# Scores for second-half queries only, another order of the seven products, and the last tile's last unit added in two column halves

## The chip, the cores and the metric

The kernel runs on one core of a Trainium2 chip. The metric is the device time of one execution in microseconds (us). A core has a matrix engine (TensorE: PE for its matmuls, PEld for its loads of the stationary operand), a vector engine (DVE), a scalar engine (ACT), a general engine (POOL) and DMA queues (SP issues most of the transfers here). Each engine works through its own instructions in the order of its program.

## The reference

One decoder layer over 512 tokens of width 1024, in float32:

```
x = LN1(ALPHA*x + 0.5*SwiGLU_1(x))           # width 2816
q, f, i, g, conv_val, conv_gate = split(x @ w_in)
f = lb + (1-lb)*sigmoid(f);  k = 1 - f        # 4 heads, state 128x128
o[t] = sum over s <= t of ( sum_c q[t,c]*k[s,c]*prod of f[r,c] for s < r <= t ) * i[s]
A = rmsnorm(o) * gain * sigmoid(g)
B = silu(LN(causal_conv31(conv_val*sigmoid(conv_gate))))
x = LN2(ALPHA*x + concat(A, B) @ w_out)
x = LN3(ALPHA*x + 0.5*SwiGLU_2(x))
```

The reference writes the recurrence chunk by chunk; the sum above is what it comes to.

## The kernel before

**Feed-forward stages.** `ffn` is called twice. Gate and up weights come as "quads" of 128 features in four 512 x 128 quarters. The first two feature blocks are computed plainly. For the other nine (f = 2 to 10), times gate and up (s = 0, 1), a `Pair` computes a 2 x 2 block product by seven products (p1 to p7) instead of eight. One product is four steps of three matmuls (L407), each with 128 x 128 weights and 256 moving columns, in the float32r type: high and low parts, three of the four cross terms. So a pair is 84 matmuls, and the two calls hold 36 pairs. The order is the tuple `USUAL`. p1, p7 and p5 open an accumulation and ACT copies their sum out of the bank (L427); p2, p4 and p3 then go on accumulating onto p1, p7 and p5, so their first weight load waits for that copy. While a pair runs, the quad of the pair after the next is prepared: ACT casts its four operands to high parts (L68), DVE takes the low parts (L76) and forms sums (L143, L149, L150). A cast goes into a weight buffer that a product of the present pair must have left: b11/b21 are used by p1 and p2, t1/t3 by p5 and p7, t4/t2 by p4 and p6, b22 (tile w2hi) by p3. PE's order is written out by hand there; the order on ACT and DVE comes from the framework's scheduler.

**Down and output projections.** `rows_out` keeps four banks (128 tokens each, 512 columns). The last four units of weights are run tile by tile, then `add` (L330, L331) adds the bank to the residual and takes statistics, and `norm` finishes the tile's layer norm.

**Scores.** `scores(hp)` handles two heads at a time (hp = 0, 1). The decays are folded into q and k level by level. First come the scores with no decay (only the diagonal is kept), then for block sizes m = 1, 2, 4, ... 64: scores of every 128-token group, 128 x 128 (`score`, L773), of which only the entries are kept whose query lies in the second half of a block of 2m and whose key lies in the first half of the same block. They are kept by DVE with a mask for m up to 8 (L781, L813 `copy_predicated` into `diag`) and by ACT copies for 16 to 64 (L816). Each level then multiplies q's second halves and k's first halves by totals of f (L805) and forms the totals of the next level (L809). m = 128 and 256 are scores between groups (L792, L796). A score is a float32 matmul, and the trace shows two records for each: 2 heads x 4 groups x 2 = 16 records in a level.

Between two levels PE is given other matmuls by `weave`: 2.6 or 1.9 us (`IDLE`) of an estimated cost, in steps of three float32r matmuls of 512 columns. For hp = 0 these are gated(2), gated(3) and rows(value), while DVE also works on the convolution (L756); for hp = 1 they are rows(gate), and from the fourth step on the conv norm (`conv_norm`: transposes, bn_stats L859, rstd by POOL, L864) is called between levels too.

Of the kernel before, what the change touches and what calls it, by code (L numbers as in the profile page):

```python
# [9 lines left out]
F32 = mybir.dt.float32  # L10
# [7 lines left out]
P = 128  # L18
# [35 lines left out]
def decoder_layer(ctx, tc, x_tok, x_q, w_first, vec, bcast, ng, w_gu1, w_d1, w_i, w_g, w_col, w_o, w_gu2, w_d2, out):  # L54
# [138 lines left out]
    def mm3(ps, lh, ll, rh, rl, first, last):  # L193
        nc.tensor.matmul(ps, lhsT=lh, rhs=rh, start=first, stop=False)  # L194
        nc.tensor.matmul(ps, lhsT=lh, rhs=rl, start=False, stop=False)  # L195
        nc.tensor.matmul(ps, lhsT=ll, rhs=rh, start=False, stop=last)  # L196
# [13 lines left out]
    masks = const.tile([P, len(MASKED) + 1, P], U8, name="masks")  # L210
# [102 lines left out]
    def rows_out(ks, per, lhs, accs, factor, late, finish, follow=(), before=lambda u: None, then=lambda: None):  # L313
# [5 lines left out]
        stats = [small.tile([P, 2, 6], F32, tag="stats", name="stats") for _ in range(NT)]  # L319

        def part(acc, u, hi, lo, i):
            for j in range(per):
                n = per * u + j
                h, l = lhs(ks[n])
                mm3(acc[i], h[:, i * P:(i + 1) * P], l[:, i * P:(i + 1) * P],
                    hi[:, j, :], lo[:, j, :], n == 0, n == len(ks) - 1)

        def add(acc, half, i):
            z = xres[i][:, half * 512:(half + 1) * 512]
            nc.vector.scalar_tensor_tensor(z, acc[i], factor, z, op0=ALU.mult, op1=ALU.add)  # L330
            nc.vector.bn_stats(stats[i][:, half, :], z)  # L331
# [22 lines left out]
        for i in range(NT):  # L354
            add(acc, 0, i)
# [84 lines left out]
    USUAL = ("p1", "p7", "p2", "p4", "p5", "p6", "p3")  # L440
# [29 lines left out]
    def ffn(x, begun, gb_i, finish, follow=(), then=lambda: None, later=lambda: None):  # L470
        with tc.tile_pool(name="ffn", bufs=1) as fp:
# [33 lines left out]
            with tc.manual_schedule(engines={PE}):  # L505
# [8 lines left out]
                for f in range(PLAIN, NP):  # L514
                    h.append(h_of(f))
                    for s in range(2):
                        ahead(3)
                        w = unit_now()
                        ahead(3)
                        pr = Pair(PAIR_BANKS[f % 2][s], work_tile() if s else h[f])  # L520
                        for n in USUAL:
                            run(pr.steps(x, w, (n,)))
                            if f == PLAIN and s == 0 and n == "p7":
                                x.last_sum()
                        gate_up(s, pr)
# [91 lines left out]
    def make_masks():  # L617
# [4 lines left out]
        for n, m in enumerate(MASKED):  # L622
# [11 lines left out]
                                    fill=0.0, base=0, channel_multiplier=0)  # L634
            nc.gpsimd.tensor_copy(masks[:, n, :], mf)
        nc.gpsimd.tensor_copy(masks[:, len(MASKED), :], ident)
# [24 lines left out]
    with tc.tile_pool(name="mix", bufs=1) as mp:  # L661
# [56 lines left out]
        def forget_query(h):  # L718
# [7 lines left out]
            def query(ps):  # L726
                nc.scalar.copy(qk[h // 2][:, 0, h % 2, :], ps)
# [3 lines left out]
        us = {}  # L731
# [32 lines left out]
        def scores(hp):  # L764
            x = qk[hp]
            xf = x.rearrange("p a h t -> p (a h t)")
            q, k = x[:, 0], x[:, 1]

            def score(n, h):
                ps = bank(nbank[h][n % 2], NT, P)  # L770
# [3 lines left out]
                return ps  # L774

            yield IDLE[hp]
            both = [score(0, h) for h in range(2)]
            f = fq[:, 2 * hp:2 * hp + 2, :]
            nc.vector.tensor_tensor(q, q, f, op=ALU.mult)
            for h in range(2):  # L780
                nc.vector.copy_predicated(diag[h], masks[:, len(MASKED):, :].broadcast_to([P, NT, P]), both[h])  # L781
            yield IDLE[hp]
            tot = f.rearrange("p h t -> p (h t)")
            for n, m in enumerate(MASKED + COPIED + (128, 256)):
                if m <= 64:
                    both = [score(n + 1, h) for h in range(2)]
                else:
                    both = [bank(nbank[h][(n + 1) % 2], NT, P) for h in range(2)]
                for h, ps in enumerate(both):
                    if m == 128:  # L790
# [3 lines left out]
                    elif m == 256:  # L794
# [11 lines left out]
                if m < 128:  # L806
                    tt = tot.rearrange("p (b two) -> p b two", two=2)
# [3 lines left out]
                for h, ps in enumerate(both):  # L811
                    if m in MASKED:
                        nc.vector.copy_predicated(diag[h], masks[:, n:n + 1, :].broadcast_to([P, NT, P]), ps)  # L813
                    elif m <= 64:
                        for b in range(0, P, 2 * m):
                            nc.scalar.copy(diag[h][b:b + m, :, b + m:b + 2 * m], ps[b:b + m, :, b + m:b + 2 * m])  # L816
# [80 lines left out]
        with tc.manual_schedule(engines={PE}):  # L897
# [12 lines left out]
            bl += [mp.tile([P, T], F32R, name=f"bl{n}") for n in range(1, NC)]  # L910
# [94 lines left out]
```

## Time and profile before

| what | value |
|---|---|
| time, median of 3 runs | 942.77 us (942.49 to 943.42) |
| the profiled execution's own time | 942.62 us |
| its span, first to last instruction | 940.6 us |
| PE busy | 931.2 us, 99% |
| DVE busy | 679.8 us, 72% |
| ACT busy | 388.2 us, 41% |
| DMA, mean | 103 GB/s |
| granted TensorE clock, mean | 0.998 of 2.4 GHz |

The profiled execution is 2.0 us longer than its span (what lies around the first and the last instruction) and 0.15 us below the median. Records of matmuls overlap, since they are pipelined: the cost of one is read from start to start, not from its duration.

### The profile page before, as it was taken

How to read it: one execution, taken by the hardware profiler on the slowest of the kernel's cores; microseconds unless marked ns; L12 is line 12 of the kernel's file. 1: busy time of each engine (PE TensorE's matmuls, PEld its weight loads, DVE VectorE, ACT ScalarE, POOL GpSimd, SP SyncE). 2: the span in 40 equal slices, each digit the busy share in tenths (PEclk: the TensorE clock that was granted, in tenths of full speed). 3: DMA queues.
4: the chain of work that ended last, by engine and by line, in shares of the span. 5: the costliest groups of instructions: out<-in, count | busy, mean ns of one | idle time of the engine just before them, and what ended most of it. 6: DMA issues, size and time to landing. Idle time of an engine off the chain costs nothing.

```text
span 940.6 us, 14283 instructions
## 1 busy us (share of the span) xinstructions
PE 931.2 (99%) x5913; PEld 844.0 (90%) x5913; DVE 679.8 (72%) x933; ACT 388.2 (41%) x560; POOL 119.3 (13%) x142
## 2 busy tenths in 40 slices
PE   9999999999999999999999999999999999999996
PEld 6899999999888889888888888989999999988885
DVE  6988888887724265999887768958888888742417
ACT  5554455555421123414341723535555544721100
POOL 0000000000820015642462201000000000000001
PEclk9999999999999999999999999999999999999999
DMA  8522322324432313321140241213233222452302
GB/s 278 202 106 90 133 92 95 131 69 146 141 106 90 94 41 101 125 71 64 48 128 5 65 168 64 109 65 115 91 102 123 90 91 90 136 156 90 98 15 89
DMA packets 22464, 96.67 MB, mean 103 GB/s; under 512 B 2496, under 2 KB 3648, under 8 KB 17024
## 3 DMA queue, kind: packets, MB, share of 16 engines
q1 hardware_dynamic: 22320, 95.50, 30.4%
q8 instruction: 46, 0.75, 0.3%
q0 software_dynamic: 80, 0.26, 0.1%
q14 instruction: 18, 0.15, 0.1%
HBM read 93.66 MB, written 2.10 MB: 102 GB/s over the span
## 4 chain that ended last, share of the span: by engine, by line
PE 98%; DVE 2%; POOL 0%; issue 0%; DVEq 0%; ACT 0%
PE bank L407 39%; PE bank L196 18%; PE bank L194 18%; PE bank L195 18%; PE bank L773 2%; PE bank L830 1%; PE bank L578 0%; PE bank L796 0%; PE bank L288 0%; PE bank L274 0%; DVE qk L805 0%; DVE diag L813 0%; PE bank L792 0%; PE bank L847 0%; DVE cn L864 0%
## 5 line engine op out<-in xcount | busy, mean ns | idle before, releaser
L76 DVE TENSOR_TENSOR wlo<-raw,whi 128x1024 fp32r<-128x1024 f32 (+2 forms) x150 | 173.5, 1163 | 148.2 <-ACT whi L68 148.1
L68 ACT CAST whi<-raw 128x1024 fp32r<-128x1024 f32 (+2 forms) x172 | 173.2, 1012 | 258.0 <-PE bank L196 150.7
L194 PE MATMUL bank<-whi,hp 128*128 128x512 f32 x320 | 124.7, 390 | 0.0
L196 PE MATMUL bank<-whi,hp 128*128 128x512 f32 x320 | 124.5, 389 | 0.0
L195 PE MATMUL bank<-wlo,hp 128*128 128x512 f32 x320 | 124.5, 389 | 0.0
L407 PE MATMUL bank<-bh,whi 128*128 128x256 f32 x432 | 122.3, 283 | 0.0
L407 PE MATMUL bank<-bl,whi 128*128 128x256 f32 x432 | 122.3, 283 | 0.0
L407 PE MATMUL bank<-ah,whi 128*128 128x256 f32 x432 | 122.2, 283 | 0.0
L407 PE MATMUL bank<-ah,wlo 128*128 128x256 f32 x432 | 122.2, 283 | 0.0
L407 PE MATMUL bank<-al,whi 128*128 128x256 f32 x432 | 122.2, 283 | 0.0
L407 PE MATMUL bank<-bh,wlo 128*128 128x256 f32 x432 | 122.1, 283 | 0.0
L756 DVE SCALAR_TENSOR_TENSOR bank<-u,vecs,bank 128x512 f32<-128x512 f32 x120 | 81.2, 748 | 2.8 <-ACT bank L751 1.8
L407 PEld LDWEIGHTS bank<-bh,whi 128*128 128x128 f32 x432 | 82.9, 192 | 0.0
L407 PEld LDWEIGHTS bank<-bl,whi 128*128 128x128 f32 x432 | 82.9, 192 | 0.0
L407 PEld LDWEIGHTS bank<-bh,wlo 128*128 128x128 f32 x432 | 82.9, 192 | 0.0
L407 PEld LDWEIGHTS bank<-al,whi 128*128 128x128 f32 x432 | 82.8, 192 | 0.1
L407 PEld LDWEIGHTS bank<-ah,whi 128*128 128x128 f32 x432 | 82.7, 192 | 0.1
L407 PEld LDWEIGHTS bank<-ah,wlo 128*128 128x128 f32 x432 | 82.8, 192 | 0.0
L222 POOL TENSOR_TENSOR rstd<-rstd,negh 128x1 f32<-128x1 f32 (+1 forms) x18 | 17.9, 997 | 497.4 <-DVE rstd L221 497.4
L76 POOL TENSOR_TENSOR wlo<-raw,whi 128x256 fp32r<-128x256 f32 x88 | 66.5, 789 | 63.3 <-ACT whi L68 61.4
L195 PEld LDWEIGHTS bank<-wlo,hp 128*128 128x128 f32 x320 | 60.1, 188 | 12.5
L196 PEld LDWEIGHTS bank<-whi,hp 128*128 128x128 f32 x320 | 60.1, 188 | 12.4
(192 smaller groups left out, 1923.2 us busy)
## 6 DMA issues: line engine op xcount, KB each, us to landing
raw<-w_gu SPq DMA_DIRECT2D x42, 1024.0 KB, 4.8
raw<-w_d SPq DMA_DIRECT2D x44, 512.0 KB, 3.5
raw<-w_col SPq DMA_DIRECT2D x16, 512.0 KB, 3.5
raw<-w_o SPq DMA_DIRECT2D x8, 512.0 KB, 3.5
xres<-x_tok SPq DMA_DIRECT2D x4, 512.0 KB, 7.9
gb<-bcast SPq DMA_DIRECT2D x4, 512.0 KB, 5.1
raw<-w_i SPq DMA_DIRECT2D x4, 512.0 KB, 3.4
raw<-w_g SPq DMA_DIRECT2D x4, 512.0 KB, 3.5
```

Source lines behind the costliest of these rows:

```text
L68: nc.scalar.copy(hi, raw)
L76: engine.tensor_tensor(lo[..., sl], raw[..., sl], hi.bitcast(F32)[..., sl], op=ALU.subtract)
L194: nc.tensor.matmul(ps, lhsT=lh, rhs=rh, start=first, stop=False)
L195: nc.tensor.matmul(ps, lhsT=lh, rhs=rl, start=False, stop=False)
L196: nc.tensor.matmul(ps, lhsT=ll, rhs=rh, start=False, stop=last)
L222: nc.gpsimd.tensor_tensor(r, r, negh.broadcast_to([P, n]) if n > 1 else negh, op=ALU.pow)
L407: nc.tensor.matmul(ps, lhsT=l[:, k, :], rhs=r[:, k, :], start=first and k == 0 and j == 0, stop=k == 3 and j == 2, skip_group_check=True)
L756: nc.vector.scalar_tensor_tensor(accs[n], us[n][:, j:j + T], vecs[:, w:w + 1], accs[n], op0=ALU.mult, op1=ALU.add)
L773: nc.tensor.matmul(ps[:, g, :], lhsT=k[:, h, sl], rhs=q[:, h, sl], start=True, stop=True)
L830: nc.tensor.matmul(ps[:, i, :], lhsT=s, rhs=v[:, j, (2 * hp + h) * P:(2 * hp + h + 1) * P], start=(j == 0), stop=(j == i))
```

## The change

**Scores.** Every level's matmul takes only the queries that the level keeps. The diagonal's scores are taken with the 64 even queries of each group only. m = 1 and m = 2 share one matmul of 128 moving columns: the odd queries (kept apart by ACT in a new tile `odd`, [.., 0, :]) and, in [.., 1, :], the queries of m = 2. From m = 4 on a matmul has 64 moving columns (the second halves' queries, a strided operand) and 128 - m stationary ones. The number of matmuls in a level stays the same; there is one level less in a pair of heads (seven instead of eight with L773's work). The mask copies (`select`) write 256 elements per partition instead of 512; the diagonal's odd entries come with the mask of m = 1, to which the identity is added. DVE gets more and smaller multiplications in the first two steps; `scores` yields ten times instead of eleven, so the first part of the conv norm comes after m = 4 instead of after m = 2, and its last part after m = 256 instead of m = 128. The query evacuation is two ACT copies of 256 columns instead of one of 512.

**Order of products.** p7, p1, p4, p5, p2, p6, p3 in every pair but those of the last feature block, which keep p1, p7, p2, p4, p5, p6, p3.

**Last tile.** In each of the three `rows_out`, the last tile's last unit is run as two column halves (12 matmuls of 256 columns for 6 of 512), and the last tile's `add` works on 256 columns at a time.

```diff
-                for n, (u, hi, lo) in enumerate(kept):
+                for n, (u, hi, lo) in enumerate(kept[:-1]):
                     part(acc, u, hi, lo, i)
...
+                for c in range(0, 512, wide[i]):
+                    part(acc, *kept[-1], i, slice(c, c + wide[i]))
...
-                add(acc, 1, i)
+                for c in range(0, 512, wide[i]):
+                    add(acc, 1, i, c)
...
-    USUAL = ("p1", "p7", "p2", "p4", "p5", "p6", "p3")
+    USUAL, LAST = ("p7", "p1", "p4", "p5", "p2", "p6", "p3"), ("p1", "p7", "p2", "p4", "p5", "p6", "p3")
...
-                        for n in USUAL:
+                        for n in USUAL if f < NP - 1 else LAST:
...
-                nc.scalar.copy(qk[h // 2][:, 0, h % 2, :], ps)
+                p2 = ps.rearrange("p (t two) -> p t two", two=2)
+                nc.scalar.copy(qk[h // 2][:, 0, h % 2, :].rearrange("p (t two) -> p t two", two=2)[:, :, 0], p2[:, :, 0])
...
+                nc.scalar.copy(odd[-1][:, h % 2, :, 0, :], p2[:, :, 1].rearrange("p (g t) -> p g t", g=NT))
...
-                    nc.tensor.matmul(ps[:, g, :], lhsT=k[:, h, sl], rhs=q[:, h, sl], start=True, stop=True)
+                    nc.tensor.matmul(ps[:, g, 0:64], lhsT=k[:, h, sl],
+                                     rhs=q[:, h, sl].rearrange("p (t two) -> p t two", two=2)[:, :, 0],
+                                     start=True, stop=True)
...
+            nc.vector.tensor_tensor(k2[..., 0], k2[..., 0], f2[..., 1], op=ALU.mult)
...
+                    nc.tensor.matmul(ps[:, g, :], lhsT=k[:, h, g * P:(g + 1) * P],
+                                     rhs=w[:, h, g].rearrange("p a t -> p (a t)"), start=True, stop=True)
...
+                    if m <= 64:
+
+                        for g in range(NT):
+                            nc.tensor.matmul(ps[0:P - m, g, 0:64].rearrange("p (b m) -> p b m", m=m),
+                                             lhsT=k[:, h, g * P:(g + 1) * P - m],
+                                             rhs=halved(q, m, 1)[:, h, g * 64 // m:(g + 1) * 64 // m],
+                                             start=True, stop=True)
...
-                        nc.vector.copy_predicated(diag[h], masks[:, n:n + 1, :].broadcast_to([P, NT, P]), ps)
+                        select(h, ps[:, :, 0:64], n, m, 1)
```

## Rows read from the trace of the kernel before

**Rows 1.** The page: busy time by engine; shares of the chain that ended last.

```profile
PE 931.2 (99%) x5913; PEld 844.0 (90%) x5913; DVE 679.8 (72%) x933; ACT 388.2 (41%) x560; POOL 119.3 (13%) x142
PE 98%; DVE 2%; POOL 0%; issue 0%; DVEq 0%; ACT 0%
```

**Rows 2.** Stretches: busy us by engine (instructions), clock, DMA share, GB/s.

```profile
49.20:232.60 183.40, 183.40 (x1514) 182.34 (x1513) 154.94 (x208) 96.52 (x145) 1.31 (x3) 1.00 0.31 106
...
489.50:529.60 40.10, 39.76 (x259) 35.24 (x258) 28.98 (x50) 12.52 (x30) 8.54 (x10) 1.00 0.09 27
```

**Rows 3.** Chain in order of time, merged: start us, us, what.

```profile
49.35 183.22 PE bank L407 x1512
...
404.01 1.78 PE bank L773 x16
...
443.87 1.73 PE bank L796 x8
```

**Rows 4.** Timeline: one level of scores with hp 0, one with hp 1.

```profile
403.85 1.95 PE L773 MATMUL bank<-m 128*128 128x128 f32 x16
...
505.43 0.39 PE L196 MATMUL bank<-whi,xl 128*128 128x512 f32 x1
...
505.88 1.86 PEld L773 LDWEIGHTS bank<-qk 128*128 128x128 f32 x16 [0.48 <-DVE qk L805]
505.88 2.05 PE L773 MATMUL bank<-qk 128*128 128x128 f32 x16
```

**Rows 5.** Timeline of the first feed-forward stage: p6 ends, p3 begins.

```profile
137.91 1.05 ACT L68 CAST whi<-t 128x1024 fp32r<-128x1024 f32 x1 [1.83 <-PE bank L407]
...
138.86 0.37 ACT L427 COPY h<-bank 128x256 f32<-128x256 f32 x1
...
139.15 0.28 PE L407 MATMUL bank<-bh,wlo 128*128 128x256 f32 x1
139.28 0.19 PEld L407 LDWEIGHTS bank<-ah,w2hi 128*128 128x128 f32 x1
...
139.39 0.19 PEld L407 LDWEIGHTS bank<-al,w2hi 128*128 128x128 f32 x1
```

**Rows 6.** Waits between engines: us in total, times, longest.

```profile
PEld bank L773 <- DVE qk L805: 1.2, 2, 0.7
```

**Rows 7.** Timeline of DVE, one masked level with hp 1, first and last.

```profile
503.99 0.73 DVE L813 COPY_PREDICATED diag<-masks,bank 128x512 f32<-128x512 uint8 x1
...
508.83 0.73 DVE L813 COPY_PREDICATED diag<-masks,bank 128x512 f32<-128x512 uint8 x1
```

**Rows 8.** Groups of DVE, shapes apart.

```profile
L813 DVE COPY_PREDICATED diag<-masks,bank 128x512 f32<-128x512 uint8 x16 | 11.7, 729 | 1.0 <-PE bank L773 1.0
...
L429 DVE TENSOR_TENSOR h<-h 128x256 f32<-128x256 f32 x18 | 7.5, 417 | 0.0
```

**Rows 9.** Timeline of ACT: the four silus that end the conv norm.

```profile
527.59 2.93 ACT L888 ACTIVATE c<-c,vecs 128x512 f32<-128x512 f32 x4
```

**Rows 10.** Groups of PE, shapes apart: busy us, mean ns of one.

```profile
L407 PE MATMUL bank<-ah,w2hi 128*128 128x256 f32 x144 | 44.2, 307 | 0.0
L407 PE MATMUL bank<-al,w2hi 128*128 128x256 f32 x144 | 40.5, 281 | 0.0
```

**Rows 11.** Timeline of ACT, first half of the pair after that.

```profile
142.45 0.37 ACT L427 COPY work<-bank 128x256 f32<-128x256 f32 x1 [0.88 <-PE bank L407]
...
143.87 0.84 ACT L492 ACTIVATE h<-h 128x768 f32<-128x768 f32 x1
144.61 0.36 ACT L427 COPY work<-bank 128x256 f32<-128x256 f32 x1
```

**Rows 12.** Chain at the end of the span.

```profile
932.56 0.24 PE bank L196
...
932.82 0.70 DVE xres L330
...
933.55 0.70 DVE stats L331
```

More of the change, by code (lines that the diff above doesn't have):

```diff
@@ L191, in decoder_layer, with mm3 @@
     plan([w_d2[h, u] for h in range(2) for u in range(NP)], tok, nc.vector)
[L193 to L196, printed above, removed]
+    def mm3(ps, lh, ll, rh, rl, first, last, **kw):
+        nc.tensor.matmul(ps, lhsT=lh, rhs=rh, start=first, stop=False, **kw)
+        nc.tensor.matmul(ps, lhsT=lh, rhs=rl, start=False, stop=False, **kw)
+        nc.tensor.matmul(ps, lhsT=ll, rhs=rh, start=False, stop=last, **kw)
     def slot(tag, shape, dtype, name):
@@ L318, in rows_out, with part @@
         n_units = len(ks) // per
-        stats = [small.tile([P, 2, 6], F32, tag="stats", name="stats") for _ in range(NT)]
-        def part(acc, u, hi, lo, i):
+        wide = [512] * (NT - 1) + [256]
+        stats = [small.tile([P, 1024 // n, 6], F32, tag=f"stats{n}", name="stats") for n in wide]
+        def part(acc, u, hi, lo, i, cols=slice(0, 512)):
             for j in range(per):
@@ L767, in scores, with banks_of, halved, select @@
             q, k = x[:, 0], x[:, 1]
-            def score(n, h):
-                ps = bank(nbank[h][n % 2], NT, P)
+            w = odd[hp]
+            turns = [0]
+            def banks_of():
+                turns[0] ^= 1
+                return [bank(nbank[h][1 - turns[0]], NT, P) for h in range(2)]
+            def halved(t, m, k):
+                return t.rearrange("p g (b two m) -> p g b two m", two=2, m=m)[:, :, :, k]
+            def select(h, ps, n, m, k):
+                r = slice(0, P - (m if m > 2 else 0))
+                mask = masks[:, n:n + 1, :].broadcast_to([P, NT, P])
+                nc.vector.copy_predicated(halved(diag[h], m, k)[r], halved(mask, m, k)[r],
+                                          ps.rearrange("p g (b m) -> p g b m", m=m)[r])
@@ L771, in score @@
+            yield IDLE[hp]
+            both = banks_of()
+            for h, ps in enumerate(both):
                 for g in range(NT):
                     sl = slice(g * P, (g + 1) * P)
-                    nc.tensor.matmul(ps[:, g, :], lhsT=k[:, h, sl], rhs=q[:, h, sl], start=True, stop=True)
-                return ps
-            yield IDLE[hp]
-            both = [score(0, h) for h in range(2)]
-            f = fq[:, 2 * hp:2 * hp + 2, :]
-            nc.vector.tensor_tensor(q, q, f, op=ALU.mult)
@@ new lines, in scores @@
+            f4, q4, k4 = (t.rearrange("p (s t r) -> p s t r", s=2 * NT, r=4)
+                          for t in (fq[:, 2 * hp:2 * hp + 2, :].rearrange("p h t -> p (h t)"),
+                                    xf[:, 0:2 * T], xf[:, 2 * T:4 * T]))
+            f2, k2 = (t.rearrange("p s t (a b) -> p s (t a) b", b=2) for t in (f4, k4))
+            tot = totals[:, 0, :]
+            w0, w1 = (w[:, :, :, i, :].rearrange("p h g (t a) -> p (h g) t a", a=2) for i in range(2))
+            t4 = tot.rearrange("p (s t a) -> p s t a", s=2 * NT, a=2)
@@ new lines, in scores @@
+            nc.vector.tensor_tensor(q4[..., 1], w0[..., 0], t4[..., 0], op=ALU.mult)
+            yield IDLE[hp]
+            both = banks_of()
+            for h, ps in enumerate(both):
+                for g in range(NT):
+                    nc.tensor.matmul(ps[:, g, :], lhsT=k[:, h, g * P:(g + 1) * P],
+                                     rhs=w[:, h, g].rearrange("p a t -> p (a t)"), start=True, stop=True)
+            two = lambda t: t.rearrange("p (b two) -> p b two", two=2)
+            nc.vector.tensor_tensor(q4[..., 2:4], w1, t4[..., 0:1].broadcast_to([P, 2 * NT, 32, 2]), op=ALU.mult)
@@ L909, in decoder_layer @@
             bl = [parts.tile([P, T], F32R, tag="w2lo", name="bl0", bufs=2)]
-            bl += [mp.tile([P, T], F32R, name=f"bl{n}") for n in range(1, NC)]
+            b12 = mp.tile([P, 2, T], F32R, tag="odd", name="bl1")
+            bl += [b12[:, 0, :], b12[:, 1, :], mp.tile([P, T], F32R, name="bl3")]
             fill = rows(gate)
```

59 lines of the change are left out of this document (36 added, 23 removed).

## Prediction

> **What bounds the kernel now.** I read the page first: PE is busy for 99% of the span, every other engine for 72% or less, and the chain that ended last runs through PE for 98% [rows 1]. So only three things can move the time: the number and pitch of PE's instructions, the short stretches in which PE waits, and the tail after its last matmul. Then the busy times by stretch: in the first feed-forward stage PE has no gap and DVE is busy 155 of 183 us, in the scores of the second pair of heads PE loses 0.3 us [rows 2]. This understates the loss, because a matmul's record can begin while its weights are still being loaded; I therefore took the cost of a matmul from start to start. The merged chain gives that pitch directly: 1512 matmuls of 256 float32r columns take 183.22 us, 0.121 each; sixteen score records of 128 float32 columns 1.78 us, 0.111 each; eight records of 256 columns 1.73 us, 0.216 each [rows 3].
>
> **Scores: columns against loads.** The pitches [rows 3] say that the pitch of a float32 record follows its moving columns, 0.108 us per 128 plus a little. Taken alone they promise half the price for 64 columns. But every score record has its own weight load, which runs beside the matmul before it, and it can hide only as long as that matmul lasts. Its length shows where nothing hides it. With hp = 1, one level's load had to wait for DVE; its first matmul's record begins with the load, and the sixteen records cover 2.05 us instead of the 1.95 of an undisturbed level: 0.10 more [rows 4]. In the feed-forward stage an exposed load of 128 columns begins at 139.28 and the next one at 139.39 [rows 5], that is, the first took 0.11 until its matmul could run. So a load of 128 float32 columns costs about 0.107 us, just what 128 moving columns hide and twice what 64 will hide (0.054). My reading: for the 64-column records the load sets the pitch, and halving the moving columns alone gains nothing.
>
> What is left of the gain is one level less, and the narrower loads from m = 4 on. Before, a pair of heads pays 8 x 1.78 = 14.24 us. After, the diagonal and the joint level (128 columns each way) cost 1.78 each. m = 4, 8, 16, 32, 64 have 124, 120, 112, 96, 64 stationary columns. No row shows a load narrower than 128, so their price lies between 1.78 (a load costs the same however narrow) and 0.89 (it is no bound, half the columns cost half). I take it in proportion to the columns, my estimate from the 0.107 for 128: 1.73 + 1.67 + 1.56 + 1.34 + 0.89 = 7.19. Four of the five are near 128 columns, so they stay near the upper row in any case. The sum is 3.56 + 7.19 = 10.75, 3.5 us less for each pair of heads, **7.0 us less** in all. The ends: with loads of constant price 7 x 1.78 = 12.46, 3.6 us less in all; with loads that are no bound 6 x 0.89 + 1.78 = 7.12, 14.2 us less in all. The strided moving operand could cost up to twice a contiguous one without leaving this, since 2 x 0.054 is the load's time again.
>
> On the narrow loads the Trainium skill (page "TensorE: Matmul & The Clock Gate", section "LDWEIGHTS (loading the stationary operand)") says that a load takes its number of columns divided by 1.2 in ns, whatever the number of rows. That gives 107 ns for 128 columns, as the exposed loads here show, and 53 ns for 64. By it the five levels come to about 7.0 us, next to my 7.19, and it speaks against the full halving, which is rival 1 below.
>
> **Scores: waits.** PE waited twice for DVE with hp = 1: its load's idle time is 1.2 us in two waits, the longer 0.7 [rows 6]. The shorter one, 0.48, holds what is usual: the load began 0.45 after the last fill matmul's start at 505.43 [rows 4], where 0.23 is one pitch of 512 columns, so 0.22 was lost. The longer one by the same subtraction loses 0.44. Each also exposes a load, 0.10. Together 0.86 us. The cause is a level in which DVE has two masked copies, the multiplications and the conv norm: from 503.99 to 508.83, 4.84 us from one level's first masked copy to the next [rows 7]. A masked copy of 512 elements takes 0.73 and an operation of 256 elements 0.42 [rows 8], so two halves give DVE about 0.62 back: 4.2 us. PE's level is then 1.67 for the scores at m = 8, nine fill matmuls of 0.23, and four transposes of about 0.11: 4.2 as well. Moreover the conv norm now begins after m = 4, so only m = 8 has both masked copies and norm. I take **0.8 us less**; the ends are 0.9 (all waits gone) and 0 (they stay).
>
> The extra DVE operations of the first two steps cost me nothing: what must lie between the diagonal's matmuls and the joint ones is only one multiplication of 512 elements (about 0.7 us), under 2.1 us of fill; the rest depends on f and the odd queries alone. If that cover went, each step would cost PE some 0.5 us, four times. The second ACT copy of each query (about 0.4 us) hides behind the 5 us of the next column unit. The conv norm's last part comes one level later: its silus take 2.93 us [rows 9], its copies and splits perhaps 3 more, and PE still has nine fill matmuls, forty records of `values` at 0.11 and the fill's leftover, some 8 us. Bound 0 to 1, taken 0.
>
> **Order of the products.** The record of p3's first high part shows the stall: its 144 matmuls average 307 ns, the neighbouring ones 281 [rows 10]. 144 x 26 ns = 3.74 us, or 0.104 for each of the 36 pairs: once per pair a load is exposed. Why: when p5 ends, ACT begins a 1.05 us cast into the buffer that p5 left (137.91), and only then copies p5's sum (138.86 to 139.23). p6 covers 12 x 0.121 = 1.45 us, its last matmul starts at 139.15, and p3's load, which waits for the copy, begins at 139.28 instead of directly behind that matmul's start [rows 5]. Lateness is 0.01 and the exposed load 0.10, 0.115 per pair. In the new order p2 and p6 lie between p5 and p3, 2.9 us, and the same copy is over a good microsecond early. What is late next? p4 follows p7 with only p1 between. A first product's copy begins 142.45, about 1.7 us after the pair's start, and ends at 142.82 [rows 11]; p4's first load is due 2.9 us after the start, at 143.6: 0.8 to spare. The second product's copy is the one behind the silus (144.61 to 144.97) [rows 11]; that is p1's now, and p2 waits for it only at 5.8 us. The last feature block keeps its order, so 32 of 36 stalls go: **3.7 us less**. Ends: 0 (the stall moves to p4) and 4.1 (all).
>
> **Last tile.** 12 matmuls of 256 columns at 0.121 for 6 of 512 at 0.227 make each unit 0.09 us longer, three times. In the first two `rows_out` PE has other work behind it, nothing else changes: +0.2. At the end DVE starts 0.26 us after the last matmul's start and takes 0.70 + 0.70 plus gaps [rows 12]; with halves of about 0.36 the first half's two operations run under the second half's matmuls, and 0.75 us stand behind the last matmul instead of 1.46, and the last matmul is shorter by 0.1. Less the 0.09 that is 0.6 to 0.7 gained. Net **0.4 us less** (0 to 0.6).
>
> **Sum.** 7.0 + 0.8 + 3.7 + 0.4 = 11.9 us. The profiled execution's own time is 942.6 (span 940.6 and 2.0 around it), 0.15 below the median of the runs, so I forecast 942.8 - 11.9 = 930.9, rounded 931.0, span near 929.
>
> **Rivals.**
> 1. Loads are no bound and half the columns cost half. For it: the pitch of 128 and 256 columns [rows 3]; against it: the exposed loads [rows 4, 5]. Scores then give 14.2 less instead of 7.0, but PE's level with hp = 1 falls to 3.4 us where DVE needs up to 4.2, which takes back about 1.2: 931.0 - 7.2 + 1.2 = 925.0.
> 2. A load costs the same however narrow: 931.0 + 3.4 = 934.4. No row excludes it.
> 3. The stall only changes its place: p4 waits for p7's copy by a hair in each pair, as p3 did: 931.0 + 3.7 = 934.7. For it: ACT's order is the scheduler's, and a cast may again go before the copy; against it: 0.8 us to spare.
> 4. Slower than before: ACT takes a cast (1.05) and the pair's silus (0.84 and the smaller one, 1.1 in all) before p7's copy. Then the copy ends 1.7 + 2.2 + 0.4 = 4.3 us after the start, p4 is 1.4 late and pays 0.1 for the load; in the 16 pairs with silus that is 24 us, in the other 16, with a cast alone, 0.4 each, 6 us: 931 + 30 = 961. It decides from 0.37 us per pair on (11.9 / 32). For it: DVE is 85% busy there [rows 2], so the silus' time may shift; against it: silus start 1.1 us after the first product's copy today [rows 11].
>
> **How the numbers follow.** Forecast 0.55, with a range of its own from 929 to 933; rival 1 0.14; rival 2 0.10; rival 3 0.12; rival 4 0.06; a mishap that I don't see and that leaves no change 0.03. The range reaches from just below rival 1 to above rival 3, 924.5 to 936.0, and leaves about 0.1 out. A measurement of this kernel tells about 0.2%, 1.9 us, from no change. All cases but the last two are faster by more: 0.91; within 0.03; slower 0.06.
>
> **What would show it.** Right: score blocks of sixteen records at 1.78 for the diagonal and the joint level and falling from 1.73 to 0.9 for m = 4 to 64; p3's first matmul no longer with a mean of its own; no PE wait on L805's successor; some 0.7 us less after the last matmul. Wrong: blocks of 0.9 us already at m = 4 (rival 1) or of 1.78 at m = 64 (rival 2); p4's first matmul with a longer mean (rivals 3 and 4); PE gaps behind DVE in the first two steps of scores.

## The result, and the profile after

| what | before | after |
|---|---|---|
| time, median | 942.76 us | 935.15 us (934.90 to 935.56) |
| ratio after / before | | 0.9919 [0.9901, 0.9936] |
| span of the profiled execution | 940.6 us | 933.1 us |
| PE busy | 931.2 us | 923.2 us |

The change makes the kernel 7.6 us faster, 4.2 us short of the forecast: inside the whole range (924.5 to 936.0), outside the 929 to 933 that the forecast had for itself. The starts of PE's matmuls in the two traces, stage by stage, say where the time came from and where some went back. The third column is the forecast's term.

| stage (matmul start to matmul start) | after - before, us | forecast |
|---|---|---|
| ahead of the first product | -0.2 | |
| seven products, two stages | -1.55, -1.56 | -3.7 |
| down projection, first stage | **+0.70** | +0.1 |
| scores hp = 0 | -2.99 | -3.5 |
| scores hp = 1 with its waits | -3.33 | -4.3 |
| transposes behind the norm of the gate | **+0.54** | 0 |
| output projection | 0.0 | +0.1 |
| down projection, second stage | **+0.91** | +0.1 |
| behind the start of the last matmul | -0.04 | -0.7 |

The page of the kernel after, busy time by engine and shares of the chain, beside [rows 1]:

```profile
PE 923.2 (99%) x5899; PEld 836.8 (90%) x5899; DVE 673.8 (72%) x953; ACT 384.1 (41%) x564; POOL 120.8 (13%) x142
PE 90%; DVE 4%; issue 3%; POOL 2%; DMA 1%; ACT 1%; DVEq 0%; POOLq 0%; ACTq 0%
```

PE is still the bound. The chain now passes through other engines for 10% instead of 2%. Partly PE really waits for DVE (below); the rest I take for work of other engines that ended just in time, since PE's busy share is the same 99%.

**The levels of the scores** stand in the chain of the kernel after (start us, us, what), hp = 0, beside the 1.78 of [rows 3]:

```profile
402.95 1.73 PE bank L807 x16
...
407.50 1.78 PE bank L831 x16
...
412.02 1.68 PE bank L849 x16
...
416.54 1.63 PE bank L849 x16
...
420.95 1.53 PE bank L849 x16
```

L807 is the diagonal (64 moving columns, 128 stationary), L831 the joint level (128 each), L849 the levels from m = 4. The diagonal moves half the columns and pays all but the full price; m = 4, 8, 16 come down with their 124, 120, 112 stationary columns. This is the picture that the forecast drew from one exposed load.

**The products.** The groups of L414 (formerly L407) for p3's high part; the numbers behind the count are the least, median and greatest duration in ns:

```profile
L414 PE MATMUL bank<-ah,w2hi x144: 283/283/385, 57.6 to 804.2; 128*128 128x256 f32 x144
L414 PE MATMUL bank<-al,w2hi x144: 277/283/283, 57.7 to 804.3; 128*128 128x256 f32 x144
```

The two have the same median, and [rows 10] showed 307 against 281 as means; 385 is the stall in the second pair of the last feature block, which keeps the old order. The first pair of that block keeps it too and has no stall any more. The second pair has a new one, where p2 begins: two steps of 0.15 and 0.22 us instead of 0.12, 0.13 us more in each stage.

**A new wait in the scores.** The chain with hp = 1 ahead of the level m = 4:

```profile
490.65 0.52 DVE qk L834
491.17 0.33 DVE totals L837
491.50 0.64 DVE diag L798
492.14 0.04 DVE rstd L221
492.17 0.74 DVE diag L798
492.91 0.53 DVE qk L835
493.44 0.04 issue
493.49 1.95 PE bank L849 x16
```

PE's level hangs on L835 (k's multiplication by the totals of m = 1 and 2), which stands behind two mask copies (L798) of the same step. From the last fill matmul's start to the level's first start 0.69 us pass instead of 0.23, so 0.46 us are lost, and the first load is exposed, 0.10 more. The groups of DVE say why; the last two numbers before the idle time are busy us and mean ns:

```profile
L798 DVE COPY_PREDICATED diag<-masks,bank 128x256 f32<-128x256 uint8 x12 | 8.5, 738 | 0.0
L798 DVE COPY_PREDICATED diag<-masks,bank 120x256 f32<-120x256 uint8 x4 | 1.7, 428 | 0.2 <-PE bank L849 0.2
L798 DVE COPY_PREDICATED diag<-masks,bank 124x256 f32<-124x256 uint8 x4 | 1.7, 428 | 0.0
```

Halving a mask copy saves time only from m = 4 on (428 ns). For the diagonal, m = 1 and m = 2, with every second element or pairs, 256 elements take 738 ns, as long as 512 did (729, [rows 8]).

**A new wait behind the values.** Timeline of POOL, and of PE's loads (rows of two answers):

```profile
530.21 1.65 POOL L222 TENSOR_TENSOR rstd<-rstd,negh 128x8 f32<-128x8 f32 x1 [14.07 <-DVE rstd L221]
531.83 1.29 POOL L726 TENSOR_TENSOR m<-m,ngb 128x512 f32<-128x512 f32 x1
...
534.11 0.53 PEld L910 LDWEIGHTS bank<-ident,m 128*128 128x128 f32 x5 [0.49 <-DVE m L906]
```

The last row of the gate reaches POOL so late that its multiplication (L726) stands behind the 1.65 us of the power for rstd (L222); DVE's L906 waits for it, and PE's transposes for DVE.

**The tail.** The chain at the end, beside [rows 12]:

```profile
925.06 0.13 PE bank L196
925.19 0.02 issue
925.22 0.76 DVE xres L333 x2
925.97 0.67 DVE stats L334 x2
926.64 0.02 issue
926.66 0.27 DVE mv L339
```

Both halves of the addition begin behind the last of the twelve matmuls: 1.43 us of DVE, before 0.70 + 0.70.

### The profile page after: what moved, and what is told of

Same layout as the page of the kernel before. It is cut to its first block, busy times and chain, and to the rows that moved or that the text cites. A ratio compares the mean times of both kernels' runs of the same rounds, so it can differ in the third digit from the quotient of the medians.

```text
span 933.1 us, 14256 instructions
## 1 busy us (share of the span) xinstructions
PE 923.2 (99%) x5899; PEld 836.8 (90%) x5899; DVE 673.8 (72%) x953; ACT 384.1 (41%) x564; POOL 120.8 (13%) x142
## 4 chain that ended last, share of the span: by engine, by line
PE 90%; DVE 4%; issue 3%; POOL 2%; DMA 1%; ACT 1%; DVEq 0%; POOLq 0%; ACTq 0%
PE bank L414 39%; PE bank L194 16%; PE bank L196 16%; PE bank L195 16%; DVE bank L771 2%; PE bank L849 1%; POOL wlo L76 1%; PE bank L274 0%; PE bank L288 0%; DMA raw<-w_g 0%; DMA xr<-x_q 0%; DVE diag L798 0%; DVE bl L954 0%; DVE m L906 0%; PE bank L920 0%
## 5 line engine op out<-in xcount | busy, mean ns | idle before, releaser
L414 PE MATMUL bank<-ah,whi 128*128 128x256 f32 x432 | 122.5, 283 | 0.0
L414 PE MATMUL bank<-bl,whi 128*128 128x256 f32 x432 | 122.3, 283 | 0.0
L414 PE MATMUL bank<-ah,wlo 128*128 128x256 f32 x432 | 122.2, 283 | 0.0
L414 PE MATMUL bank<-al,whi 128*128 128x256 f32 x432 | 122.2, 283 | 0.0
L414 PE MATMUL bank<-bh,whi 128*128 128x256 f32 x432 | 122.2, 283 | 0.0
L414 PE MATMUL bank<-bh,wlo 128*128 128x256 f32 x432 | 122.2, 283 | 0.0
L414 PEld LDWEIGHTS bank<-ah,whi 128*128 128x128 f32 x432 | 82.9, 192 | 0.2
L414 PEld LDWEIGHTS bank<-bh,whi 128*128 128x128 f32 x432 | 82.9, 192 | 0.1
L414 PEld LDWEIGHTS bank<-bl,whi 128*128 128x128 f32 x432 | 82.9, 192 | 0.1
L414 PEld LDWEIGHTS bank<-bh,wlo 128*128 128x128 f32 x432 | 82.9, 192 | 0.0
L414 PEld LDWEIGHTS bank<-al,whi 128*128 128x128 f32 x432 | 82.9, 192 | 0.0
L414 PEld LDWEIGHTS bank<-ah,wlo 128*128 128x128 f32 x432 | 82.9, 192 | 0.0
L222 POOL TENSOR_TENSOR rstd<-rstd,negh 128x1 f32<-128x1 f32 (+1 forms) x18 | 16.8, 935 | 509.4 <-DVE rstd L221 509.4
L76 POOL TENSOR_TENSOR wlo<-raw,whi 128x256 fp32r<-128x256 f32 x88 | 69.4, 821 | 61.1 <-ACT whi L68 59.1
```

The lines of the kernel that those rows point to most:

```text
L76: engine.tensor_tensor(lo[..., sl], raw[..., sl], hi.bitcast(F32)[..., sl], op=ALU.subtract)
L222: nc.gpsimd.tensor_tensor(r, r, negh.broadcast_to([P, n]) if n > 1 else negh, op=ALU.pow)
L414: nc.tensor.matmul(ps, lhsT=l[:, k, :], rhs=r[:, k, :], start=first and k == 0 and j == 0, stop=k == 3 and j == 2, skip_group_check=True)
```

## The experiments

| label | median, us | ratio to before [95%] | span |
|---|---|---|---|
| e1_scores_only | 937.09 | 0.9942 [0.9929, 0.9954] | 935.7 |
| e2_order_only | 939.21 | 0.9966 [0.9952, 0.9979] | 937.2 |
| e3_last_tile_only | 944.85 | 1.0022 [1.0014, 1.0031] | 942.9 |
| e4_pad | 934.16 | 0.9911 [0.9897, 0.9924] | 932.7 |
| e5_cols (one run) | 937.16 | | 935.2 |
| e6_k_by_head | 935.78 | 0.9931 [0.9918, 0.9945] | 933.7 |
| e7_fill_first | 933.01 | 0.9898 [0.9885, 0.9912] | 930.9 |
| e8_tail_bank | 933.44 | 0.9903 [0.9890, 0.9917] | 931.4 |
| e9_all_three | 932.62 | 0.9893 [0.9876, 0.9909] | 930.8 |
| e10_more_fill | 932.34 | 0.9891 [0.9877, 0.9906] | 930.7 |
| e11_mix_aligned | 932.21 | 0.9888 [0.9873, 0.9903] | 930.1 |
| e12_all_five | 931.64 | 0.9881 [0.9864, 0.9897] | 929.5 |

Lines such as L835 are those of each run's own kernel, and so shift a little between runs.

**e1, e2, e3: one part at a time.** e1 is the kernel after without the new order and the halves; e2 and e3 are the kernel before with the new order, or with the new `rows_out`, alone:

```diff
# e1, against after
-    USUAL, LAST = ("p7", "p1", "p4", "p5", "p2", "p6", "p3"), ("p1", "p7", "p2", "p4", "p5", "p6", "p3")
+    USUAL, LAST = ("p1", "p7", "p2", "p4", "p5", "p6", "p3"), ("p1", "p7", "p2", "p4", "p5", "p6", "p3")
-        wide = [512] * (NT - 1) + [256]
+        wide = [512] * NT
...
# e2, against before
-                        for n in USUAL:
+                        for n in USUAL if f < NP - 1 else LAST:
...
# e3, against before
+                for c in range(0, 512, wide[i]):
+                    part(acc, *kept[-1], i, slice(c, c + wide[i]))
...
```

Expected of e1:

> The scores' part of the change alone, with the old order of products and the old last tile. If the three parts act by themselves, the stage of scores gives what the changed kernel's trace shows between its milestones: 3.0 us less with the first two heads, 3.3 less with the other two, 0.5 lost again in the wait before the transposes of the normalized output: 5.8 less, 937.0 us. If a part of the shortfall comes from the parts' interplay (another order on ACT and DVE), the time lies elsewhere, near 935.0 when the scores alone give the 7.8 us that were forecast for them.

Expected of e2:

> The new order of products alone. From the milestones of the changed kernel's trace: 1.55 us less in each feed-forward stage, 3.1 in all, 939.7 us. By the forecast's term: 3.7 less, 939.1 us. If the stall only moved: 942.8.

Expected of e3:

> The last tile's column halves alone. Theory: the halves gain nothing at the end (the first half's add waits for the second half's matmuls) and cost about 0.1 us in each of the three stages; and their larger statistics tiles push the tiles behind them by 384 bytes per partition, so that two of the stationary tiles of the down projection no longer stand at the same address modulo 256 bytes as the moving weights, which costs 0.55 us in the first and 0.65 to 0.8 in the second feed-forward stage: slower by 1.3 to 1.6, 944.1 to 944.4 us, with steps of 230 to 241 ns in two units of each pass. Rival (the address is no matter): slower by 0.2, 943.0 us, all steps 227.

e1: hp = 0 -2.99 us, as in the whole change; hp = 1 -2.74 (its wait ahead of m = 4 is 0.96 and not 0.46), the transposes +0.5, the down projections 0.00. So that last wait comes from the scores, and the down projections' loss does not. The products, in the old order, take 0.19 and 0.17 us more than in the kernel before; why stays open. e2: -1.55 in each stage of products, less than 0.1 anywhere behind the first product otherwise. e3: +0.71 and +0.91 in the down projections, where twelve matmuls for six account for 0.1 and 0.2. (Its profiled execution has another 0.4 us ahead of the first product, where e11's has as much; no part of the change acts there.) The last tile's halves make the kernel slower by 0.2%.

**e4: the same with other addresses.** In the trace of after the extra time of the down projections is not in the halves. It is spread over steps of 228 to 241 ns in a few units: in the first of them 384 of 485 steps of 512 columns take 226 or 227 ns, where before 480 do. The new statistics tiles are 96 bytes for 48, four buffers of each size, and move all tiles allocated behind them. By the addresses in the built program, some stationary tiles thereby stand 128 bytes off a multiple of 256 from the moving weights; in the first stage the 97 steps into or out of their matmuls average 232.5 ns, all others 226.9. e4 makes the tiles larger and restores the distance:

```diff
-        stats = [small.tile([P, 1024 // n, 6], F32, tag=f"stats{n}", name="stats") for n in wide]
+        stats = [small.tile([P, 12 if n == 512 else 32], F32, tag=f"stats{n}", name="stats")[:, 0:6 * 1024 // n]
+                 .rearrange("p (a b) -> p a b", b=6) for n in wide]
```

> The changed kernel with 32 bytes more in each of the four statistics tiles of the last tile's shape (128 per partition in all), so that the tiles behind them stand at the old address modulo 256 bytes relative to the weights. Theory: all steps of the down projections back at 227 ns, 1.2 us less than the changed kernel, 933.9 us. Rival (address is no matter, the slow steps have another cause): 935.1 us.

Measured: down projections +0.07 and +0.18 against before, that is 0.63 and 0.73 us less than in after. The chain of the kernel after, twelve steps, first and last and the two longest:

```profile
842.10 0.23 PE bank L194
...
842.79 0.24 PE bank L194
...
844.42 0.24 PE bank L195
...
844.89 0.23 PE bank L194
```

and of e4, twelve steps:

```profile
841.95 0.23 PE bank L195
...
844.67 0.23 PE bank L195
```

2.79 us against 2.72, at the same work. The span is only 0.4 less, because e4's profiled execution waits longer elsewhere: 0.95 us ahead of m = 4, 0.5 more than after's, and 0.43 more at the start of p2 in the second stage's last pair.

**e5: stationary or moving columns.** With hp = 0 every level loads all 128 stationary columns; with hp = 1 the loads stay narrow and the moving columns go from 64 to 32 (the first of each group, so that m = 4 to 64 of that pair of heads are left out of the result).

```diff
-                            nc.tensor.matmul(ps[0:P - m, g, 0:64].rearrange("p (b m) -> p b m", m=m),
-                                             lhsT=k[:, h, g * P:(g + 1) * P - m],
+                            if hp == 0:
+                                nc.tensor.matmul(ps[:, g, 0:64].rearrange("p (b m) -> p b m", m=m),
+                                                 lhsT=k[:, h, g * P:(g + 1) * P],
...
+                            else:
+                                nc.tensor.matmul(ps[0:P - m, g, 0:32],
+                                                 lhsT=k[:, h, g * P:(g + 1) * P - m],
+                                                 rhs=q[:, h, g * P:g * P + 32], start=True, stop=True)
```

> Based on the padded version. What sets the pitch of a score record, the load of its stationary columns or its moving columns? With the first two heads, m = 4 to 64 keep all 128 stationary columns (64 moving); with the other two heads they keep the narrowed stationary operand, but only 32 columns move (the wrong ones, and the results of these levels are left out). Load theory: the first two heads' five levels all last as long as the diagonal's, 1.70 us from first to last start, instead of 1.65, 1.60, 1.50, 1.30, 1.08; the other heads' levels stay at 1.63, 1.53, 1.33, 1.08 for m = 8 to 64. Moving theory: the first two heads' levels do not change, the other two heads' fall to half of theirs or less.

Timeline of e5: m = 64 with hp = 0 (128 stationary and 64 moving columns), m = 32 and 64 with hp = 1 (96 and 64 stationary, 32 moving):

```profile
429.42 1.89 PE L851 MATMUL bank<-m 128*128 128x64 f32 x16
...
508.89 1.47 PE L856 MATMUL bank<-qk 128*96 128x32 f32 x16
513.26 1.12 PE L856 MATMUL bank<-qk 128*64 128x32 f32 x16
```

and of e4, the same two levels with hp = 0 and 64 moving columns:

```profile
424.49 1.49 PE L850 MATMUL bank<-m 128*96 128x64 f32 x16
428.73 1.15 PE L850 MATMUL bank<-m 128*64 128x64 f32 x16
```

Half the moving columns take 0.02 or 0.03 off a level; twice the stationary ones add 0.74. The load sets the pitch: from its second step on a level steps at 112 ns with 128 stationary columns, 85 with 96 and 58 with 64, and the last two are the same whether 64 or 32 columns move. Only a level's first step follows the moving columns, 55 ns with 64 and 28 with 32 (m = 64 apart, whose first step is 106 and 80). That is all that the half of the columns saves. The Trainium skill (page "TensorE: Matmul & The Clock Gate", section "LDWEIGHTS (loading the stationary operand)") gives the columns divided by 1.2 in ns: 107, 80, 53. The trace agrees in the slope, and each step is 5 ns longer.

**e6: k's multiplication head by head.** PE's wait ahead of m = 4 hangs on L835 behind two mask copies; e6 splits it so that the first head's part might go ahead.

```diff
-            nc.vector.tensor_tensor(k4[..., 0:2], k4[..., 0:2], t4[..., 1:2].broadcast_to([P, 2 * NT, 32, 2]), op=ALU.mult)
+            for h in range(2):
+                s = slice(NT * h, NT * (h + 1))
+                nc.vector.tensor_tensor(k4[:, s, :, 0:2], k4[:, s, :, 0:2], t4[:, s, :, 1:2].broadcast_to([P, NT, 32, 2]), op=ALU.mult)
```

> Based on the padded version. After the joint level of m = 1 and 2, k is multiplied one head at a time (two operations of 256 elements for one of 512). Theory: PE's wait before m = 4 with the last two heads (0.45 us in the changed kernel's trace, 0.95 in the padded one's) comes from mask copies of the first head, of 0.72 us each, that DVE takes up before the multiplication of k, because that one needs both heads' matmuls; with one operation per head the wait goes and 0.5 to 1.0 us with it: 933.2 to 933.7 us. Rival: DVE has too much work in that step in any order; the wait stays above 0.3 us and the time at 934.2.

It came out slower than e4. The wait ahead of m = 4 is gone, as the theory had it, and one of 1.8 us stands ahead of m = 8. Timeline of e6, DVE, then POOL:

```profile
493.96 0.20 DVE L221 TENSOR_SCALAR rstd<-ss 128x8 f32<-128x8 f32 x1
494.19 0.73 DVE L799 COPY_PREDICATED diag<-masks,bank 128x256 f32<-128x256 uint8 x1
497.20 0.35 DVE L909 SCALAR_TENSOR_TENSOR m<-m,rstd,m 128x128 f32<-128x128 f32 x1 [2.27 <-POOL m L727]
497.47 0.42 DVE L799 COPY_PREDICATED diag<-masks,bank 124x256 f32<-124x256 uint8 x1
...
494.26 1.65 POOL L222 TENSOR_TENSOR rstd<-rstd,negh 128x8 f32<-128x8 f32 x1 [5.16 <-DVE rstd L221]
495.88 1.28 POOL L727 TENSOR_TENSOR m<-m,ngb 128x512 f32<-128x512 f32 x1
```

The scheduler moved the small L221 behind the mask copies: 493.96 for 491.81 in e4, 1.5 us later when both are counted from the start of the scores with hp = 1. On it hangs POOL's power, on that the gate, and DVE's gate multiplication L909 is queued ahead of the mask copies of m = 4, so that DVE itself stands idle for 2.27 us. e6 therefore doesn't decide between its theory and its rival: the split took the one wait away, and another order on DVE, which I hadn't asked for, brought the other.

**e7, e8, e9: two mends and all three.** e7 runs the last two fill steps (gate rows) ahead of the values:

```diff
             run(norm)
-            values(1)
             run(fill)
+            values(1)
```

e8 gives the second half of the last tile's last unit a bank of its own, and only at the kernel's end; two additions bring it together:

```diff
-                for c in range(0, 512, wide[i]):
-                    add(acc, 1, i, c)
...
+                add(acc, 1, i, 0)
+                if cut:
+                    z = xres[i][:, 768:1024]
+                    nc.vector.scalar_tensor_tensor(z, acc[i][:, 256:512], factor, z, op0=ALU.mult, op1=ALU.add)
+                    nc.vector.scalar_tensor_tensor(z, more[:, 0:256], factor, z, op0=ALU.mult, op1=ALU.add)
...
```

Both are built on e4; e9 has them together.

> Based on the padded version. The two fill steps that one yield less leaves over are run before the last values matmuls instead of behind them. Theory: the last gate row then reaches ACT and POOL 4 us earlier, POOL multiplies it before the pow of the last rstd, and PE's wait before the transposes of the normalized output (0.42 us and an exposed load of 0.1) goes: 933.7 us. Rival: what holds the transposes back is the conv norm's last part on ACT and DVE; the wait stays or moves to the first unit of the output projection, 934.2 us.

> Based on the padded version. Only the last feed-forward stage halves its last tile's last unit, and the second column half of that unit goes to a bank of its own, which DVE adds afterwards; the other two stages keep whole columns. Theory: DVE now works while PE runs the second half, since no one writes the bank it reads; 0.6 to 0.7 us less behind the last matmul, and 0.2 less in the three stages: 933.3 us. Rival: the additional addition and the smaller operations eat it up: 934.0 us.

> The changed kernel with the three mends together: the wide statistics tiles (placement), the gate rows' last two fill steps ahead of the values, the last half of the last tile of the second feed-forward stage summed in a bank of its own. Theory (the three are independent: they act at the output of rows_out, ahead of the transposes, and behind the last matmul): the one with the first two gave 933.0 us, the tail adds 0.3 to 0.4, so 932.6, and no wait ahead of the transposes. Rival (the tail's gain was a difference between two executions): 933.0.

e7: the transposes wait no longer (-0.49 us against e4), and the stage behind the scores is back at before's length within 0.01. e8: the first half's addition now runs under the second half's matmuls. DVE's timeline of e9 at the end, where the first half's last matmul ends at 922.41 in its chain and the second half's last one starts at 922.84:

```profile
922.44 0.42 DVE L334 SCALAR_TENSOR_TENSOR xres<-bank,xres 128x256 f32<-128x256 f32 x1 [0.29 <-PE bank L196]
922.78 0.41 DVE L391 SCALAR_TENSOR_TENSOR xres<-bank,xres 128x256 f32<-128x256 f32 x1
923.11 0.41 DVE L335 BATCH_NORM_STATS2 stats<-xres 128x6 f32<-128x256 f32 x1
923.44 0.41 DVE L392 SCALAR_TENSOR_TENSOR xres<-bank,xres 128x256 f32<-128x256 f32 x1
923.88 0.43 DVE L393 BATCH_NORM_STATS2 stats<-xres 128x6 f32<-128x256 f32 x1
924.35 0.26 DVE L340 BATCH_NORM_AGGREGATE mv<-stats 128x2 f32<-128x24 f32 x1
```

From the last matmul's start to the span's end e8 and e9 take 0.25 us less than e4, not the 0.6 to 0.7 of the forecast, since the second bank costs an addition more. That pays for the 0.18 that the halves cost in that stage and little else. e9 came out at 932.62, as expected of independent mends.

**e10, e11, e12: the cover in the scores, the placement elsewhere.** e10 is e9 with one fill step moved ahead of m = 4 for hp = 1; e11 is e9 with the output projection's stationary tiles at a multiple of 256 bytes from the moving weights; e12 has both.

```diff
-            yield IDLE[hp]
+            yield IDLE[hp] + (0.65 if hp else 0.0)
...
-            us[n] = mp.tile([P, T + CW - 1], F32, tag=f"u{n}", name="u")
+            us[n] = mp.tile([P, 576], F32, tag=f"u{n}", name="u")[:, 0:T + CW - 1]
-            al = [mp.tile([P, T + CW - 1], F32R, tag=f"u{h}", name=f"al{h}")[:, 0:T] for h in range(NH)]
+            al = [mp.tile([P, 576], F32R, tag=f"u{h}", name=f"al{h}")[:, 0:T] for h in range(NH)]
-        ss = mp.tile([P, NH, NT], F32, name="ss")
+        ss = mp.tile([P, 64], F32, name="ss")[:, 0:NH * NT].rearrange("p (a b) -> p a b", a=NH)
```

> The same with one more fill step (three matmuls of 512 columns, 0.68 us) between the joint scores and those of m = 4 with hp = 1; the step is taken from the two that ran ahead of the values, so PE's work is unchanged. Theory (with hp = 1 DVE has up to 0.5 us more work in that one step than PE has fill, and less than PE's fill in the steps behind it): the wait ahead of m = 4 (0.45 to 0.95 us, and 0.10 of exposed load) goes, 0.5 to 0.7 us less than the kernel with the three mends. Rival 1 (DVE is behind by a debt that the later steps do not pay back): the wait comes back ahead of m = 8, as it did when k's multiplication was split by head, and the time is unchanged. Rival 2 (the last gate row needs both steps ahead of the values): a wait of 0.3 or more comes back ahead of the transposes.

> The kernel with the three mends, and in the mix stage the conv inputs' tiles take 576 floats instead of 542 and the sums of squares 64 floats instead of 16, so that all stationary tiles of the output projection stand a multiple of 256 bytes from its moving weights (six of the eight low parts stood 64 bytes off such a multiple). No work changes. Theory (placement modulo 256 bytes between the two operands costs a matmul of 512 columns some 14 ns): the 40 slow steps of the output projection (240 to 244 ns instead of 226 or 227) go, 0.55 to 0.7 us less than the kernel with the three mends. Rival (the slow steps there come from something else, such as DVE or DMA traffic in that stage, which is the same): unchanged within 0.1 us, and the 40 steps stay.

> The three mends, the fill step moved ahead of m = 4, and the mix stage's tiles placed a multiple of 256 bytes from the output projection's moving weights. Theory (the two last act in different stages and add up): against the kernel with three mends, whose profile has a span of 930.8, 0.3 to 0.4 less in the scores with hp = 1 and 0.7 less in the output projection, so a median of 931.6 to 932.0, and neither the wait ahead of m = 4 nor a step of 240 ns in the output projection. Rival (both gains are the same slack, given back at a later wait): 932.3.

e10: the wait ahead of m = 4 is gone; in e9 it took 0.48 us from start to start, about as in after, and 0.10 of exposed load. But 0.2 come back ahead of m = 256, where DVE's multiplication (L880) comes behind a gate multiplication (L918) that had waited 0.43 us for POOL. So the scores with hp = 1 are only 0.37 us shorter for the expected 0.5 to 0.7; the transposes are unchanged. The difference of the medians (0.28) lies within the spread of the runs, and so may the stage's: e11, without the step, waits just 0.17 us there in its profiled execution, and its scores with hp = 1 are 0.31 shorter than e9's. e11: the output projection is 0.68 us shorter. Of the 147 steps of 512 columns between `values` and the next operand's transposes (L288), 138 take 226 or 227 ns, where e9 has 27 such; the time beyond 226.8 ns in the steps up to 241 falls from 0.70 us to 0.05. The chain of e9 in that stage:

```profile
560.21 0.23 PE bank L194
560.44 0.24 PE bank L195
560.67 0.24 PE bank L196
560.91 0.24 PE bank L194
```

and of e11:

```profile
560.23 0.23 PE bank L196
560.46 0.23 PE bank L194
560.68 0.23 PE bank L195
560.91 0.23 PE bank L196
```

e12 has both in its trace (hp = 1 -3.93 against before up to the end of `values`, output projection -0.68) and the lowest median, 931.64 us. What the fill step adds is less sure: e11, without it, already has -3.89 with hp = 1.

## Why the prediction was right, and where it fell short

That the number lies in the range is partly luck: 935.15 lies beside the prices of rivals 2 and 3 (934.4 and 934.7), for whose sake the range reaches so far, and neither of them happened. Instead each of the five terms below fell short, by 0.5 to 1.9 us.

**Scores, -7.0.** The mechanism was right and rivals 1 and 2 are refuted by e5. The size was 6.1, twice what hp = 0 shows: with both neighbouring fill steps, less their undisturbed 0.227 each, the seven levels take 1.79, 1.79, 1.74, 1.70, 1.59, 1.39 and 1.28, together 11.27 us for a forecast 10.75, and before 8 x 1.79. Three quarters of the difference are m = 64, 1.28 for 0.89: 0.04 by its pitch (58 ns for the forecast's 55.6), the rest at the level's borders. The step ahead of it takes 0.32 instead of 0.23, its first step 0.106 instead of 0.055, and 0.49 pass between its last start and that of the second fill matmul, where other levels have 0.35 to 0.40. I did not try why. The prediction's "about 7.0 us" for the five narrow levels, by the load time that the Trainium skill (page "TensorE: Matmul & The Clock Gate", section "LDWEIGHTS (loading the stationary operand)") gives, is 6.9 when it is summed (16 records for each level, 516 columns in the five). They measured 7.70.

**Waits, -0.8.** The two old waits did go: the step into a level behind m = 4 takes 0.23 us in after (0.32 at m = 64), where before two took 0.44 and 0.67. The step that failed is "two halves give DVE about 0.62 back". It was priced from the number of elements; for the diagonal, m = 1 and m = 2 it is nothing, and these are the levels that the change had put together. "What must lie between the diagonal's matmuls and the joint ones is only one multiplication" was right about that gap; I did not ask the same of the next one, where DVE has three multiplications and four mask copies under the same 2 us of fill. It costs 0.56 in the profiled execution of after, and between 0.3 and 1.1 in those of the other runs that have it, since single DVE operations of this stretch differ between executions (below).

**"Taken 0" for the conv norm.** The norm itself was hidden. What the bound of 0 to 1 held was something else: one yield less leaves two fill steps behind the values, and the gate's last row is late by POOL's power. +0.5 us, shown by e7.

**Order, -3.7.** Right in mechanism, 3.1 in size. Before, the two steps at p3's start take 0.135 and 0.223 us, 0.118 more than two usual ones and close to the forecast's 0.115; but the steps behind them run 1 to 3 ns short and give 0.02 back, so that a pair falls only from 10.18 us to 10.08. 34 pairs lose the stall, two more than forecast, and the new stall of p2 in each stage's last pair takes 0.26 back, which the forecast put at nothing. Rivals 3 and 4 did not come: in the new order no product has a stall.

**Last tile, -0.4.** It came out at +1.5. First, "with halves the first half's two operations run under the second half's matmuls" was wrong in this program: both halves share a bank, and only the last of the twelve matmuls carries the signal that DVE waits for. With a bank of its own (e8) they do run there. Second, "nothing else changes" in the down projections: larger statistics tiles moved other tiles, +1.36 us (e4). The 0.09 for twelve matmuls was right (0.07; 0.18 in the last unit, where the count ends at the start of a shorter matmul).

So the 4.2 us between forecast and result are 0.9 in the scores, 0.5 in the waits, 0.6 in the order, 0.5 in the gate and 1.9 in the last tile, less 0.2 ahead of the first product.

## What to carry to other kernels

Before cutting a matmul's moving columns, look for one exposed weight load in the trace: in a run of matmuls with a load each it was the floor of the pitch here, and only fewer stationary columns lowered it. When a step's work is merged with another's, list again what stands on the helping engine in that step, each with the row of its own access pattern; half the elements are not half the time. After an edit that only adds a small tile, compare the pitch of matmuls that it doesn't touch.

## What the hardware showed that I had not expected

**Placement.** A float32r matmul of 512 columns whose stationary tile is 128 (down projections) or 64 (output projection) bytes off a multiple of 256 from its moving operand mostly has steps of 228 to 241 ns; where all distances of a stage are multiples of 256, nearly all its steps take 226 or 227. The distances are read from the built programs, and it was shown in both directions (after and e4, e9 and e11). Which distance modulo which size costs how much was not mapped out, and the reason stays open.

**Access patterns on DVE.** In after's timeline a multiplication of 256 elements with hp = 1 takes 0.42 us at a step of two elements (L820) and 0.62 to 0.68 at a step of four (L821, L824, L825). The Trainium skill (page "SBUF — State Buffer", section "Specifications (TRN2)") tells of lines of 16 bytes and of full rate only with at least two hits in a line, which is a step of two for float32; the trace agrees for the multiplications. It doesn't explain the mask copies: with a step of two, 256 elements take 0.738 us.

**DVE beside POOL.** The same multiplication of 256 elements (L822 of e4, L833 of e9) took 1.16 us in one execution and 0.61 in another; in both POOL subtracted low parts in the same microseconds. Which DVE operation is stretched differs between executions, and with it, it seems, the wait ahead of m = 4 (0.17 to 0.96 us). That POOL is the cause is not shown: I made no run that separates them.

**The clock behind a wait.** In e5, behind PE's wait ahead of m = 4, the granted clock of 494.0 to 499.5 us was 0.71, and fill steps went at 0.43 us instead of 0.23: the lower of the two levels (1.2 of 2.4 GHz) for a part of the stretch. PE had been idle for 0.8 us and busy with short matmuls before. It need not have fallen by that wait: e4 lost 0.95 us at the same place and e6 1.8 ahead of m = 8, and there it stayed at 1.00. What made the difference, no run here shows.
